# One trunk layer on one core: the unrounded activations rebuilt by a sum, three low parts by transfer instead of four, two weight units split by VectorE, the keys' transposes in other PSUM banks, the rotary tables' products at a later place

## The chip, the cores and the metric

The kernel runs on one core of one Trainium2 chip. The metric is the device time in microseconds of one execution; three runs of the kernel before gave 826.57 (the median), 824.71 and 828.17. All times below are of the kernel before. Engine names are those of the profile: PE is TensorE's matrix multiplication, PEld its load of the stationary operand, DVE is VectorE, ACT ScalarE, POOL GpSimd, and SP the engine whose queue issues most loads.

## The reference

One layer of an encoder over 512 positions of width 1024, in float32. Cut to what matters:

```python
h = rmsnorm(x, pre_mix_g)
aq, ak, av, hq, hf_fwd, hf_bwd, hi, hg = split_columns(h @ w_in, IN_SPLITS)
att = axial_gqa_attention(apply_rope(rmsnorm(aq)), apply_rope(rmsnorm(ak)), av)   # 8 heads of 64, 2 of keys
rec = hgrn2_group(hq, hf_fwd, hf_bwd, hi, hg, lb, out_g)                          # 4 heads, a gated scan both ways
x = x + rmsnorm(concat([att, rec]) @ w_out, post_mix_g)
h = rmsnorm(x, pre_x_g);  m = rmsnorm(mem, mem_norm_g)                            # 256 memory rows
x = x + rmsnorm(memory_cross_attention(h, m, w_xq, w_xkv, w_xo), post_x_g)
h = rmsnorm(x, pre_ffn_g)
u = conv3(h @ w_up) + conv_b                                                      # 1024 -> 2 x 2816
x = x + rmsnorm((silu(u_gate) * u_val) @ w_down, post_ffn_g)
```

## The kernel before, in words

**Products.** A float32 product is put together from three faster ones. Each operand is split into a rounded part "hi" (type fp32r) and a rest "lo", and `mm3` (L243 to L245) issues hi·hi, hi·lo and lo·hi into the same PSUM bank. PSUM has eight banks, handed out by four tags, `b`, `s`, `c`, `o`, two banks each. A tag's third request waits until the first one's bank has been read for the last time.

**Splitting.** `split` (L118, L119) casts the source to hi on ACT and subtracts on DVE. For activations the source is mostly a PSUM bank, so that bank stays taken until DVE's subtraction has read it.

**Weights.** Weights come in units of 128x1024 numbers. `issue` loads a unit into a `raw` buffer on SP's queue and makes its `wh` and `wl`, up to three units ahead of the one that PE uses. For most units that is `split`. For units in `NEG_SCALAR` (7 to 30) ACT casts (L212), ACT writes the negative of the rounded part into `wl` (L214), and a transfer issued by POOL (L217) adds the unit from DRAM on top of it, so DVE has nothing to do there. For units in `NEG_POOL` POOL does the negation (L216). Units 7 to 10 are those of the recurrent group's output gate, `put_sg`, which is the first of `mix_projections`.

**Streams.** `weave` interleaves generators: first the projections (`mix_projections`, with `hgrn_in` for each recurrent head) and the cores of heads 0 to 2 (`hgrn_core`), then the core of head 3 with the self-attention and the cross-attention's key projections. A core goes through its levels: an ACT copy (L604), four small products on PE (L607), two in-place updates on DVE (L633), and a masked copy (L639). Each engine has one fixed order of instructions, made when the kernel is built, and takes them in that order; an instruction that waits holds up all behind it on that engine.

**Rotary tables.** `rope_tables` scales the loaded cosines and sines by the rows' norms (four ACT products, L671) and multiplies them with the gains of queries and keys (four DVE products, L674 and L676). They are first used when the queries are normalized, at 175.5 us. `mem_turn`, the transposition of the normalized memory, ends at about 135 us.

**Keys.** `turn_k(b)` transposes one block of 128 keys on PE (L715) into a bank of tag `b`, from which ACT copies it (L716). The cross-attention's key projections, which run at the same time, also take their banks from `b`. Blocks 0 and 1 are turned after key projection 1, blocks 2 and 3 after key projection 2. The attention's scores (L830) need all four.

**Up-projection.** `between` norms the rows after the cross-attention; its `turn_in` transposes a block of rows into two banks (L282), splits both (L118, L119) and, for this stage only, copies both once more to an unrounded buffer `fulls` (L289). The first two columns' products (`us`) run beside the last transpositions. Later columns i = 5, 8, 11, 14 and 17 go through `strassen_pair`, which needs four sums of quarters of the unrounded input (`sum_of_h`, L1080, and a `split` each), made at i = 2 and 3, one after each product. A pair's four weight units are the loaded `diag` and `side` and two sums of those (`add_blocks`, L188 to L194).

**Down-projection.** Seven products of sums run one after the other, each over three groups of columns. `left_side(p, g)` makes the left operand of product p and group g: for pairs in `NEG_GROUP`, which is group 1 of products 1, 2, 5 and 6, ACT casts (L1022), POOL negates (L1023) and a transfer of POOL's adds the source (L1024); for all others `split` does it. Ahead of product 3 DVE overwrites a source in place (L1014).

Of the kernel before, what the change touches and what calls it, by code (L numbers as in the profile page):

```python
# [9 lines left out]
F32 = mybir.dt.float32  # L10
# [3 lines left out]
ACT = mybir.ActivationFunctionType  # L14
# [4 lines left out]
P = 128  # L19
D = 1024  # L20
T = 512
NB = T // P
# [15 lines left out]
UP_PRODUCTS = ("w11", "w22", "t2", "w21", "t1", "t3", "t4")  # L38
LAY_AHEAD, LOAD_AHEAD = 3, 5
SIDES_AT = (18, 19)  # L40
NEG_GROUP = frozenset((p, 1) for p in (1, 2, 5, 6))
AHEAD = 3
HOLD_BLOCK = 4
TURN_STEP, MEM_TURN, UP_TURN = 0, (0, 4), (0, 2)
NEG_SCALAR = frozenset(range(7, 31))
NEG_POOL = frozenset(range(31, 42))
CORE_SHARE, ATT_LEAD = 53.0, 4.0
KEY_TURNS = {1: (0, 1), 2: (2, 3)}
# [38 lines left out]
def layer(tc, io, out):  # L87
    nc = tc.nc
# [16 lines left out]
    def bank(tag):  # L105
        return ps.tile([P, 512], F32, name="ps_" + tag, tag=tag)

    def big(shape, dt=F32):
        return b8.tile(shape, dt, name="big", tag="big")
# [137 lines left out]
    def blk(b):  # L247
        return slice(b * P, (b + 1) * P)
# [26 lines left out]
        nc.vector.scalar_tensor_tensor(out=h[:, half(c)], in0=xb[:, half(c)], scalar=r, in1=g[:, half(c)],  # L275
                                       op0=ALU.mult, op1=ALU.mult)

    def turn_in(h, act, b, tags, keep=None):
        for c in range(2):
            o = bank(tags[c]).rearrange("p (k n) -> p k n", k=4)  # L280
            for k in range(4):
                nc.tensor.transpose(o[:, k, :], h[:, blk(c * 4 + k)], ident)  # L282
            hi, lo = act.hi, act.lo
            if len(hi) == 2:
                split(hi[c][:, :, blk(b)], lo[c][:, :, blk(b)], o)
            else:
                split(hi[0][:, c * 4:c * 4 + 4, blk(b)], lo[0][:, c * 4:c * 4 + 4, blk(b)], o)
            if keep:
                nc.scalar.copy(keep[c][:, :, blk(b)], o)  # L289

    def row_rstd(xb, h):
        ss = small()
# [13 lines left out]
        nc.vector.scalar_tensor_tensor(out=xb[:, cols], in0=yg, scalar=ss[:, R:R + 1], in1=xb[:, cols],  # L306
                                       op0=ALU.mult, op1=ALU.add)

    def between(x, g_post, g_pre, act, keep=None):
        def first(b, y):  # L310
            ss = small()
            return ss, residual_part(ss, y, g_post, 0, half(0), False, "th")

        def second(b, got, y):
            h = tmp4([P, D])
            ss = small()
            got = got[0], (got[1], residual_part(got[0], y, g_post, 1, half(1), True))
            for c in range(2):
                residual_add(got[0], got[1][c], x[b])
                nc.scalar.activation(h[:, half(c)], x[b][:, half(c)], ACT.Square, accum_out=ss[:, c:c + 1])  # L320
                rstd_part(ss, c, c == 1)
            for c in range(2):
                scale_rows(x[b], ss[:, R:R + 1], g_pre, h, c)
            return lambda: turn_in(h, act, b, y_tags[0][b] + y_tags[1][b], keep)
        return first, second

    def new_act():
# [106 lines left out]
    hT = new_act()  # L434
# [96 lines left out]
    def pair(act, i):  # L531
        t = big([P, 2, 2, T], F32R)
        act.hi[i], act.lo[i] = t[:, 0], t[:, 1]
    sg_box, heads, qkv, rec_done = [], {}, {}, [0]

    def put_v(b, o):
        nc.scalar.mul(v[:, b, :], o, r[:, b:b + 1])
# [17 lines left out]
    def hgrn_in(h, between=()):  # L555
        qk = big([P, 2, 2, T])
        tt = big([P, 2048])
        q = tmp2(tag="tq")

        def put_q(z):  # L560
            nc.scalar.activation(q, z, ACT.Sigmoid)
            nc.vector.tensor_mul(q, z, q)

        def put_f(d):
            def put(z):
                f = tt[:, d * T:(d + 1) * T]
                k = qk[:, 1, d, :]
                nc.scalar.activation(f, z, ACT.Sigmoid)
                nc.scalar.activation(k, z, ACT.Sigmoid, scale=-1.0)
                nc.scalar.activation(f, f, ACT.Identity, scale=oml[:, d, h:h + 1], bias=lb[:, d, h:h + 1])  # L570
                nc.vector.scalar_tensor_tensor(out=qk[:, 0, 1 - d, :], in0=f, scalar=oml[:, d, h:h + 1], in1=q,
                                               op0=ALU.mult, op1=ALU.mult)
            return put

        for put in (put_q, put_f(0), put_f(1)):
            yield from proj_fm(hT, T, "b", scaled(put))
            for job in between[:3]:
                job()
            between = between[3:]
        heads[h] = (q, qk, tt)  # L580
# [86 lines left out]

    def rope_tables():
        rope, cs = qkv["tables"][:, 0:4], qkv["tables"][:, 4:6]
        for b in range(NB):  # L670
            nc.scalar.mul(cs[:, :, b, :], cs[:, :, b, :], r[:, b:b + 1])  # L671
        nc.vector.tensor_scalar(qkg[:, 0, :], qkg[:, 0, :], 0.125, None, op0=ALU.mult)
        for i in range(2):
            nc.vector.tensor_mul(rope[:, 2 * i], cs[:, 0], qkg[:, None, i, :].to_broadcast([P, NB, 64]))  # L674
            gs = pat(qkg, i * 64 + 1, [[0, NB], [2, 32], [-1, 2]])
            nc.vector.tensor_tensor(out=rope[:, 2 * i + 1].rearrange("p b (i two) -> p b i two", two=2),  # L676
                                    in0=cs[:, 1].rearrange("p b (i two) -> p b i two", two=2), in1=gs, op=ALU.mult)
        return rope
# [30 lines left out]
                                in1=kd[:, :, 0].bitcast(F32), op=ALU.subtract)  # L709

    def turn_k(b):
        o = bank("b").rearrange("p (k n) -> p k n", k=4)
        kd4 = qkv["kd"][:, b].rearrange("p a b c d -> p (a b) (c d)")
        for i in range(4):
            nc.tensor.transpose(o[:, i, :].bitcast(F32R), kd4[:, i, :], ident_r)  # L715
        nc.scalar.copy(qkv["kT"][:, :, blk(b)], o)  # L716
# [263 lines left out]

    g_post, g_pre = gains("post_x_g", "pre_ffn_g")
    hT = new_act()
    fulls = [big([P, 4, T]) for _ in range(2)]
    turns = res_second(ox, range(4), kv["x0"], between(x, g_post, g_pre, hT, fulls))

    acts, sides, gates, last_act = [], [], {}, [None]
    half_t = [slice(0, 256), slice(256, 512)]
# [75 lines left out]
    for part in range(2):  # L1063
        cols = slice(part * 256, part * 256 + 256)
        for n in range(4):
            for kc in range(8):
                mm3(us[n][:, cols], (ws[n][0][:, kc, :], ws[n][1][:, kc, :]), hT.get(kc, cols), kc == 0, kc == 7)
            if part:
                conv(*first[n], us[n])
            elif n in UP_TURN:  # L1070
                turns.popleft()()
    wide = [big([P, 2, 4, 256]) for _ in range(2)]
    s1, s2, s3, s4 = wide[0][:, 0], wide[0][:, 1], wide[1][:, 0], wide[1][:, 1]
    (a11, a21), (a12, a22) = [[f[:, :, t] for t in half_t] for f in fulls]
    sums_of_h = [(t[:, 0], t[:, 1]) for t in (big([P, 2, 4, 256], F32R) for _ in range(4))]
    of_h = [(s1, a21, a22), (s2, a11, s1), (s3, a21, a11), (s4, a12, s2)]

    def sum_of_h(k):
        o, i0, i1 = of_h[k]
        nc.vector.tensor_sub(o, i0, i1)  # L1080
        split(*sums_of_h[k], o)
# [43 lines left out]
    for i in range(2, NF):  # L1125
        if i in UP_S:
            strassen_pair(i)
        else:
            for c in range(2):
                o = next_bank()  # L1130
                w = unit(8)
                for kc in range(8):
                    mm3(o, (w[0][:, kc, :], w[1][:, kc, :]), hT.get(kc, slice(0, T)), kc == 0, kc == 7)
                conv(c, i, o)
                if i < 4:
                    sum_of_h(2 * i - 4 + c)
        if i % 3 == 2 and i // 3 < 6:
            new_sums(i // 3)

# [173 lines left out]
```

## Time and profile before

| what | value |
|---|---|
| three runs, median (lowest to highest) | 826.57 us (824.71 to 828.17) |
| the profiled execution | 825.72 us, of it a span of 823.8 us |
| granted TensorE clock, mean | 0.999 |
| busy: PE, PEld | 808.1 us (98%), 690.6 us (84%) |
| busy: DVE, ACT, POOL | 568.5 (69%), 473.0 (57%), 132.3 (16%) us |
| transfers issued by POOL into `wl` (L217) | 35 of 512 KB, 5.4 us to landing (median) |
| copies L289 | 8 of 128x512, 0.59 us each, between 460.3 and 483.2 us |

The span is counted from the first instruction to the last. In a row of the timeline stand the start, the duration, engine, line, operation, tiles and shapes, and in square brackets the idle time of that engine before it with what ended it. In the chain of waits a row is start, duration and what the end of the program was waiting for at that moment.

### The profile page before, as it was taken

To read this page: it belongs to the slowest core of one execution; us is meant where nothing else is said; L and a number is where in the kernel's file an instruction comes from. 1 tells how busy PE (TensorE), PEld (TensorE's weight loads), DVE (VectorE), ACT (ScalarE), POOL (GpSimd) and SP (SyncE) were. 2 spreads that over 40 slices of the span, in tenths; PEclk is the share of its full clock that TensorE was granted. 3 is DMA by queue.
4 is the path that set the end of the run, shared out by engine and by line. 5 is a ranking of instruction groups with operands and counts; after the bars stand their busy time and mean duration, and the time that the engine had idled before them with its cause. 6 is when DMAs were issued, how large, how long until landed. Compare 5 with 4: busy or idle time off the path is not lost.

```text
span 823.8 us, 11495 instructions
## 1 busy us (share of the span) xinstructions
PE 808.1 (98%) x4354; PEld 690.6 (84%) x4354; DVE 568.5 (69%) x849; ACT 473.0 (57%) x785; POOL 132.3 (16%) x194
## 2 busy tenths in 40 slices
PE   9999999999999999999999999999999999999996
PEld 7878888889898887888888898889889888878884
DVE  5347486569886875855453769787687796868865
ACT  6666756369788874645543665444344453556651
POOL 0110211044233101300001300111110102100302
PEclk9999999999999999999999999999999999999999
DMA  9696753657668533252212145787898885368842
GB/s 316 186 283 134 173 112 95 129 140 162 160 155 191 116 136 120 77 179 78 88 43 101 37 163 153 205 232 202 224 279 217 232 250 146 103 200 295 249 124 102
DMA packets 39671, 135.66 MB, mean 165 GB/s; under 512 B 5120, under 2 KB 6656, under 8 KB 39424
## 3 DMA queue, kind: packets, MB, share of 16 engines
q1 hardware_dynamic: 25632, 86.03, 30.0%
q0 software_dynamic: 10960, 40.38, 25.5%
q10 hardware_dynamic: 3024, 8.53, 2.9%
q8 instruction: 34, 0.56, 0.3%
q14 instruction: 21, 0.17, 0.1%
HBM read 130.72 MB, written 25.17 MB: 189 GB/s over the span
## 4 chain that ended last, share of the span: by engine, by line
PE 84%; DMA 4%; DVE 4%; issue 3%; ACT 2%; POOL 2%; SPq 0%; POOLq 0%; DVEq 0%; ACTq 0%
PE ps_b L243 9%; PE ps_b L244 9%; PE ps_b L245 9%; PE ps_s L244 6%; PE ps_s L245 6%; PE ps_s L243 6%; PE ps_o L243 5%; PE ps_o L245 5%; PE ps_o L244 5%; PE ps_c L245 4%; PE ps_c L244 4%; PE ps_c L243 4%; PE ps_c L607 3%; PE ps_o L851 2%; PE ps_s L830 2%
## 5 line engine op out<-in xcount | busy, mean ns | idle before, releaser
L119 DVE TENSOR_TENSOR wl<-raw,wh 128x1024 fp32r<-128x1024 f32 (+1 forms) x75 | 90.7, 1212 | 64.1 <-ACT wh L118 63.8
L118 ACT CAST wh<-raw 128x1024 fp32r<-128x1024 f32 (+1 forms) x75 | 76.8, 1027 | 83.0 <-PE ps_b L244 25.7
L243 PE MATMUL ps_b<-big,wh 128*128 128x512 f32 (+1 forms) x340 | 122.4, 360 | 0.7 <-DVE big L119 0.7
L245 PE MATMUL ps_b<-big,wl 128*128 128x512 f32 (+1 forms) x340 | 120.5, 355 | 0.0
L244 PE MATMUL ps_b<-big,wh 128*128 128x512 f32 (+1 forms) x340 | 120.5, 354 | 0.0
L243 PEld LDWEIGHTS ps_b<-big,wh 128*128 128x128 f32 x340 | 64.3, 189 | 9.2 <-DVE big L119 0.9
L244 PEld LDWEIGHTS ps_b<-big,wh 128*128 128x128 f32 x340 | 64.3, 189 | 8.6
L245 PEld LDWEIGHTS ps_b<-big,wl 128*128 128x128 f32 x340 | 64.2, 189 | 8.7
L633 DVE TENSOR_TENSOR big<-big 128x512 f32<-128x512 f32 x64 | 48.4, 761 | 16.4 <-PE ps_c L607 10.1
L244 PE MATMUL ps_s<-wl,big 128*128 128x512 f32 (+1 forms) x140 | 53.4, 381 | 2.6 <-DVE wl L119 1.7
L243 PE MATMUL ps_s<-wh,big 128*128 128x512 f32 (+1 forms) x140 | 53.5, 384 | 0.4 <-DVE big L119 0.4
L245 PE MATMUL ps_s<-wh,big 128*128 128x512 f32 (+1 forms) x140 | 53.1, 379 | 0.0
L212 ACT CAST wh<-raw 128x1024 fp32r<-128x1024 f32 x35 | 36.8, 1052 | 26.7 <-PE ps_b L244 12.9
L217 POOL DMA_DIRECT2D wl<-in_w_dram x35 | 30.9, 883 | 120.1 <-ACT wl L214 105.1
L119 DVE TENSOR_TENSOR big<-ps_o,big 128x512 fp32r<-128x512 f32 x54 | 37.0, 688 | 14.1 <-ACT big L118 12.2
L998 POOL DMA_DIRECT2D sum_t<-in_wd_dram x24 | 19.7, 833 | 143.7 <-DMA sum_t<-in_wd_dram 86.8
L118 ACT CAST big<-ps_o 128x512 fp32r<-128x512 f32 x54 | 31.6, 589 | 17.2 <-PE ps_o L953 7.5
L243 PE MATMUL ps_o<-wh,big 128*128 128x512 f32 (+1 forms) x102 | 39.3, 386 | 0.0
L244 PE MATMUL ps_o<-wl,big 128*128 128x512 f32 (+1 forms) x102 | 38.2, 375 | 0.0
L245 PE MATMUL ps_o<-wh,big 128*128 128x512 f32 (+1 forms) x102 | 38.2, 374 | 0.0
L244 PE MATMUL ps_c<-big,wh 128*128 128x256 f32 (+1 forms) x112 | 37.6, 336 | 0.0
L243 PE MATMUL ps_c<-big,wh 128*128 128x256 f32 (+1 forms) x112 | 37.6, 336 | 0.0
(311 smaller groups left out, 2171.0 us busy)
## 6 DMA issues: line engine op xcount, KB each, us to landing
raw<-in_w_dram SPq DMA_DIRECT2D x85, 512.0 KB, 3.3
wl<-in_w_dram POOLq DMA_DIRECT2D x35, 512.0 KB, 5.4
sum_t<-in_wd_dram POOLq DMA_DIRECT2D x20, 512.0 KB, 8.1
tmp<-in_w_dram SPq DMA_DIRECT2D x14, 512.0 KB, 6.0
sum_t<-in_wd_dram ACTq DMA_DIRECT2D x10, 512.0 KB, 6.2
sum_t<-sum_t POOLq DMA_DIRECT2D x10, 512.0 KB, 5.2
big<-sum_t SPq DMA_DIRECT2D x10, 512.0 KB, 4.9
raw<-sum_t SPq DMA_DIRECT2D x10, 512.0 KB, 4.5
```

The lines of the kernel that those rows point to most:

```text
L118: nc.scalar.copy(hi, src)
L119: (eng or nc.vector).tensor_sub(lo, src, hi.bitcast(F32))
L212: nc.scalar.copy(wh, raw)
L217: nc.gpsimd.dma_start(wl, io["w"][i], accum_op=ALU.add)
L243: nc.tensor.matmul(o, a[0], b[0], start=start, stop=False, skip_group_check=again)
L244: nc.tensor.matmul(o, a[0], b[1], start=False, stop=False, skip_group_check=again)
L245: last_mm[0] = nc.tensor.matmul(o, a[1], b[0], start=False, stop=stop, skip_group_check=again).ins
L607: nc.tensor.matmul(o[:, b, :], kc[:, blk(b)], pat(qk, b * P, [[2 * m, P // (2 * m)], [T + m, 2], [1, m]]), start=True, stop=True)
L633: nc.vector.tensor_tensor(out=c, in0=c, in1=pat(tt, toff + off, [[2, npair], [gap, 2], [0, m]]), op=ALU.mult)
L830: nc.tensor.matmul(s, qT[h // 4][:, h % 4, blk(qb)], kT[:, 2 * (h // 4) + c, :], start=c == 0, stop=c == 1)
L851: nc.tensor.matmul(o, vv[:, c, h // 4].rearrange("p a d -> p (a d)"), pt[j][:, c, :], start=c + j == 0, stop=c == 3 and j == 1)
L998: nc.gpsimd.dma_start(t, weight_block(second_name, width(u)), accum_op=ALU.add)
```

## The change

Five edits go together:

- `turn_in` no longer copies to `fulls`; `full_h(c)` makes each half of `fulls` later by one DVE sum of the hi and lo parts, 128x2048, at i = 2. The four `sum_of_h` all move to i = 3, two after each product.
- `NEG_GROUP` loses product 1, so that its group 1 is split by ACT and DVE.
- `NEG_SCALAR` begins at 9, so that units 7 and 8 are split by ACT and DVE.
- The four ACT products of the rotary tables are recorded behind the newest forget gate's last activation (L570), and DVE's four follow them.
- `turn_k` takes its bank from the tags `s`, `s`, `o`, `o` of the blocks' own projections.

```diff
-NEG_GROUP = frozenset((p, 1) for p in (1, 2, 5, 6))
+NEG_GROUP = frozenset((p, 1) for p in (2, 5, 6))
...
-NEG_SCALAR = frozenset(range(7, 31))
+NEG_SCALAR = frozenset(range(9, 31))
...
     def turn_in(h, act, b, tags, keep=None):          # loses the argument keep
...
-            if keep:
-                nc.scalar.copy(keep[c][:, :, blk(b)], o)
...
-                nc.scalar.activation(f, f, ACT.Identity, scale=oml[:, d, h:h + 1], bias=lb[:, d, h:h + 1])
+                last_gate[0] = nc.scalar.activation(f, f, ACT.Identity, scale=oml[:, d, h:h + 1],
+                                                    bias=lb[:, d, h:h + 1]).ins
...
-        for b in range(NB):
-            nc.scalar.mul(cs[:, :, b, :], cs[:, :, b, :], r[:, b:b + 1])
+        with tc.issue_after(last_gate[0]):
+            for b in range(NB):
+                nc.scalar.mul(cs[:, :, b, :], cs[:, :, b, :], r[:, b:b + 1])
...
     def turn_k(b):
-        o = bank("b").rearrange("p (k n) -> p k n", k=4)
+        o = bank(tm_tags[b]).rearrange("p (k n) -> p k n", k=4)
...
+    def full_h(k):
+        nc.vector.tensor_add(fulls[k], hT.hi[k].bitcast(F32), hT.lo[k].bitcast(F32))
...
                 conv(c, i, o)
-                if i < 4:
-                    sum_of_h(2 * i - 4 + c)
+                if i == 2:
+                    full_h(c)
+                elif i == 3:
+                    sum_of_h(2 * c)
+                    sum_of_h(2 * c + 1)
```

The buffers `fulls` are now taken behind the first two columns instead of ahead of them. The edits also shift line numbers: in the changed file L606 is the line that was L607, L603 that was L604, L1079 is `full_h`, L1083 the sum in `sum_of_h` that was L1080, and L1039, L1041 and L1052 the convolution's lines that were L1040, L1042 and L1053.

On PE, around the keys' transposes, the order before is this, from the end of key projection 1 (L243 to L245) to the start of projection 2, and then from the end of projection 2 to the scores, with part of projection 3 left out between:

```order
L245 MATMUL ps_b<-big,wl 128x256
L715 MATMUL ps_b<-ident_r,big 128x128 x4
L607 MATMUL ps_c<-big,tmp_1932 128x128 x4
L715 MATMUL ps_b<-ident_r,big 128x128 x4
L243 MATMUL ps_b<-big,wh 128x256
...
L715 MATMUL ps_b<-ident_r,big 128x128 x4
L607 MATMUL ps_c<-big,tmp_2090 128x128 x4
L715 MATMUL ps_b<-ident_r,big 128x128 x4
...
L830 MATMUL ps_s<-big 128x512 x4
```

And this is the same stretch of PE's order in the changed kernel:

```order
L245 MATMUL ps_b<-big,wl 128x256
L715 MATMUL ps_s<-ident_r,big 128x128 x6
L606 MATMUL ps_c<-big,tmp_1930 128x128 x4
L715 MATMUL ps_s<-ident_r,big 128x128 x2
L243 MATMUL ps_b<-big,wh 128x256
...
L715 MATMUL ps_o<-ident_r,big 128x128 x8
...
L830 MATMUL ps_s<-big 128x512 x4
...
L606 MATMUL ps_c<-big,tmp_2088 128x128 x4
```

The transposes left tag `b` and stand closer together; the core's small products that stood between the second pair of blocks now follow the scores.

On DVE, at the columns i = 2 and 3 of the up-projection, the order before begins with the end of column 1's convolution (L1053) and goes on with the sums of quarters (L1080), their low parts (L119 to `big`), the weights' low parts (L119 to `wl`) and the weights' sums (L188, L190):

```order
L1053 TENSOR_TENSOR big<-tmp_4663,tmp_4692 128x512
L1080 TENSOR_TENSOR big<-big 128x1024
L188 TENSOR_TENSOR both<-raw 128x1024
L1040 SCALAR_TENSOR_TENSOR tmp_4734<-ps_b,cw,tmp_4734 128x511
L119 TENSOR_TENSOR wl<-tmp_4445,wh 128x1024
L1042 SCALAR_TENSOR_TENSOR tmp_4734<-ps_b,cw,tmp_4734 128x511
L119 TENSOR_TENSOR big<-big 128x1024
...
L194 TENSOR_TENSOR tmp_4877<-raw 128x512
L1053 TENSOR_TENSOR big<-tmp_4824,tmp_4864 128x512
L119 TENSOR_TENSOR wl<-both,wh 128x1024
```

The changed kernel's DVE has there, from the same convolution on:

```order
L1052 TENSOR_TENSOR big<-tmp_4651,tmp_4680 128x512
L1079 TENSOR_TENSOR big<-big 128x2048
L1039 SCALAR_TENSOR_TENSOR tmp_4724<-ps_b,cw,tmp_4724 128x511
L119 TENSOR_TENSOR wl<-tmp_4437,wh 128x1024
L1041 SCALAR_TENSOR_TENSOR tmp_4724<-ps_b,cw,tmp_4724 128x511
L1079 TENSOR_TENSOR big<-big 128x2048
L188 TENSOR_TENSOR both<-raw 128x1024
...
L1083 TENSOR_TENSOR big<-big 128x1024
L1052 TENSOR_TENSOR big<-tmp_4810,tmp_4853 128x512
L119 TENSOR_TENSOR big<-big 128x1024 x2
L119 TENSOR_TENSOR wl<-raw,wh 128x1024
L194 TENSOR_TENSOR tmp_4869<-raw 128x512
```

The two long sums came in ahead of everything else at i = 2, and the last sums' low parts now stand behind column 3's convolution, ahead of the `side` unit's low part and of L194.

On ACT, the rotary products stand before between copies of the first core, at the profile's 64 us:

```order
L604 COPY tmp_540<-big 128x512
L214 ACTIVATE wl<-wh 128x1024
L604 COPY tmp_557<-big 128x512
L671 ACTIVATE big<-big,rx 128x2x64 x4
L604 COPY tmp_580<-big 128x512
```

In the changed kernel ACT has them behind the casts of the turned memory (L118), in front of the copies of the core of head 2 (L597 and L603, which were L598 and L604):

```order
L118 CAST big<-ps_o 128x4x128
L671 ACTIVATE big<-big,rx 128x2x64 x4
L214 ACTIVATE wl<-wh 128x1024
L122 ACTIVATE big<-ps_c,og 128x512
L597 COPY big<-ps_c 128x4x128
L603 COPY tmp_1208<-big 128x512
```

DVE's four products moved with them, from between the first core's updates to behind the low parts of the turned memory. On PE the first L607 of that core stands five products later than before, 17 instead of 12 behind the core's first products (L597).

More of the change, by code (lines that the diff above doesn't have):

```diff
@@ L276, in scale_rows, with turn_in @@
                                        op0=ALU.mult, op1=ALU.mult)
-    def turn_in(h, act, b, tags, keep=None):
+    def turn_in(h, act, b, tags):
         for c in range(2):
@@ L307, in residual_add, with between @@
                                        op0=ALU.mult, op1=ALU.add)
-    def between(x, g_post, g_pre, act, keep=None):
+    def between(x, g_post, g_pre, act):
         def first(b, y):
@@ L323, in second @@
                 scale_rows(x[b], ss[:, R:R + 1], g_pre, h, c)
-            return lambda: turn_in(h, act, b, y_tags[0][b] + y_tags[1][b], keep)
+            return lambda: turn_in(h, act, b, y_tags[0][b] + y_tags[1][b])
         return first, second
@@ L533, in pair @@
         act.hi[i], act.lo[i] = t[:, 0], t[:, 1]
-    sg_box, heads, qkv, rec_done = [], {}, {}, [0]
+    sg_box, heads, qkv, rec_done, last_gate = [], {}, {}, [0], [None]
     def put_v(b, o):
@@ L982, in layer @@
     hT = new_act()
-    fulls = [big([P, 4, T]) for _ in range(2)]
-    turns = res_second(ox, range(4), kv["x0"], between(x, g_post, g_pre, hT, fulls))
+    turns = res_second(ox, range(4), kv["x0"], between(x, g_post, g_pre, hT))
     acts, sides, gates, last_act = [], [], {}, [None]
@@ L1071, in layer @@
                 turns.popleft()()
+    fulls = [big([P, 4, T]) for _ in range(2)]
     wide = [big([P, 2, 4, 256]) for _ in range(2)]
```

## The prediction, made before the changed kernel was run

> **What bounds the kernel now.** I read the page first, for the span, the busy shares and the chain that ended last.
>
> ```profile
> span 823.8 us, 11495 instructions
> PE 808.1 (98%) x4354; PEld 690.6 (84%) x4354; DVE 568.5 (69%) x849; ACT 473.0 (57%) x785; POOL 132.3 (16%) x194
> PE 84%; DMA 4%; DVE 4%; issue 3%; ACT 2%; POOL 2%; SPq 0%; POOLq 0%; DVEq 0%; ACTq 0%
> ```
>
> PE is busy for 98% of the span and carries 84% of the chain. The change takes no product off PE; it can gain only where PE waits. So I went through PE's timeline for starts later than the usual step, which is 0.23 us from one 128x512 matmul to the next (52.08 and 52.31 below) and 0.12 for 128x256, and then read the other engines and the chain of waits around each. "Excess" below is the start minus the previous start minus that step. Five of the longer gaps lie at the edits' places, and each edit has its own.
>
> **Units 7 and 8 split by DVE.** The timeline of PE, ACT, POOL and DVE, and one piece of the chain of waits (start, length, what):
>
> ```profile
> 39.46 0.69 DVE L542 TENSOR_TENSOR tmp<-ps_b,big 128x512 f32<-128x512 f32 x1 [3.55 <-PE ps_b L245]
> 41.70 1.04 ACT L214 ACTIVATE wl<-wh 128x1024 fp32r<-128x1024 f32 x1
> 44.00 0.75 DVE L571 SCALAR_TENSOR_TENSOR big<-big,oml,tmp 128x512 f32<-128x512 f32 x1 [2.95 <-ACT big L570]
> ...
> 43.06 8.41 DMA wl<-in_w_dram
> ...
> 50.14 0.39 PE L243 MATMUL ps_s<-wh,big 128*128 128x512 f32 x1
> 51.52 0.50 PE L244 MATMUL ps_s<-wl,big 128*128 128x512 f32 x1 [0.98 <-DMA wl<-in_w_dram]
> 52.08 0.40 PE L243 MATMUL ps_s<-wh,big 128*128 128x512 f32 x1
> 52.31 0.40 PE L244 MATMUL ps_s<-wl,big 128*128 128x512 f32 x1
> ```
>
> PE stood from 50.37 to 51.52 (excess 51.52 - 50.14 - 0.23 = 1.15) for the low part of unit 8, whose transfer took 8.41 us. The change replaces ACT's 1.04 us and the transfer, for two units, by a 128x1024 subtraction on DVE (1.22 us, the row at 730.37 below). DVE idles 3.55 us ahead of 39.46 and 2.95 ahead of 44.00, which covers one each; unit 8's low part is then there by about 43, 8 us early. If that cover were gone, the subtractions would delay the gates behind them by 2.4 us, less than those 8. POOL's queue and the transfers lose 1 MB, so the next unit's part comes no later. Gain between 0.4 (the next unit's transfer ends last in its place) and 1.15; I take 1.0. A rule of the Trainium skill speaks against this term: "DMA: Bandwidth & Descriptors", section on the anatomy of one DMA on the gpsimd path, gives about 2.0 us plus the bytes at 436 GB/s, an estimate of 3.2 us for 512 KB. By it neither this wait nor that of product 1 below would exist; the rows of 8.41 and 8.46 us decide against it, and what it would give is the fourth rival.
>
> **Product 1's low part by DVE.** Timeline and one piece of the chain:
>
> ```profile
> 717.64 1.94 POOL L1023 TENSOR_SCALAR big<-big 128x1024 fp32r<-128x1024 f32 x1 [17.22 <-ACT big L1022]
> 718.59 1.53 DVE L119 TENSOR_TENSOR wl<-raw,wh 128x512 fp32r<-128x512 f32 x1
> 719.88 8.46 DMA big<-big
> 722.31 1.21 DVE L119 TENSOR_TENSOR wl<-big,wh 128x1024 fp32r<-128x1024 f32 x1
> 728.36 1.23 DVE L1014 TENSOR_TENSOR big<-big 128x1024 f32<-128x1024 f32 x1 [4.83 <-DMA big<-big]
> 729.50 0.95 DVE L119 TENSOR_TENSOR big<-big 128x768 fp32r<-128x768 f32 x1
> 730.37 1.22 DVE L119 TENSOR_TENSOR wl<-raw,wh 128x1024 fp32r<-128x1024 f32 x1
> 731.64 0.50 PE L244 MATMUL ps_s<-wl,big 128*128 128x512 f32 x1 [1.66 <-DVE wl L119]
> ```
>
> DVE's update in place at 728.36 had to wait until the transfer had read its source, and behind it stood the weights' low part that PE wanted at 729.8. In the changed order one more 1.22 us subtraction stands on DVE and the wait is gone: from 722.31 with 1.13 us from one such row to the next, three of them and one of 0.87 more, the weights' low part is ready near 727, about 3 us early. PE's excess here is 1.82, of it 1.66 idle. Bounds 0.8 (another transfer of the same queue ends late) and 1.82; I take 1.8, since nothing but that wait held DVE.
>
> **Keys' transposes in other banks.** PE and ACT:
>
> ```profile
> 208.64 0.54 PE L715 MATMUL ps_b<-ident_r,big 128*128 128x128 f32 x4 [0.22 <-ACT big L716]
> 209.93 0.39 PE L243 MATMUL ps_b<-big,wh 128*128 128x256 f32 x1 [0.75 <-DVE big L119]
> 213.88 1.05 ACT L212 CAST wh<-raw 128x1024 fp32r<-128x1024 f32 x1
> 215.74 0.54 PE L715 MATMUL ps_b<-ident_r,big 128*128 128x128 f32 x4 [0.51 <-ACT big L716]
> 216.31 0.59 ACT L716 CAST big<-ps_b 128x512 fp32r<-128x512 f32 x1
> ```
>
> With both transposes and the projection on tag `b`, PE waited three times for a bank: excess 0.39, 0.88 and 0.67, together 1.94. In `s` and `o` the banks are those of blocks normalized long before, and the `b` bank that projection 2 takes was last read for projection 0. New is that the scores come sooner behind the last transposes: by the order 13 products of 0.12, 1.56 us, stand between, while ACT has two copies of 0.59 to do and, if its cast of 1.05 stands ahead as at 213.88, needs 2.2. A wait of some 0.6 can come of that, and at worst the last of the three comes back with it, so the gain lies between 0.7 and 1.94; I take 1.8.
>
> **Unrounded input by a sum.** ACT, PE, DVE, with the chain's first such piece at 463.54:
>
> ```profile
> 463.54 0.55 ACT big L289
> ...
> 468.93 0.59 ACT L289 COPY big<-ps_b 128x512 f32<-128x512 f32 x1
> 469.53 0.59 ACT L289 COPY big<-ps_s 128x512 f32<-128x512 f32 x1
> 479.06 0.66 PE L282 MATMUL ps_c<-ident,tmp 128*128 128x128 f32 x4 [0.48 <-ACT big L289]
> 479.43 0.69 DVE L119 TENSOR_TENSOR big<-ps_o,big 128x512 fp32r<-128x512 f32 x1
> 480.15 0.59 ACT L289 COPY big<-ps_o 128x512 f32<-128x512 f32 x1 [1.15 <-DVE big L119]
> 480.79 0.39 PE L243 MATMUL ps_o<-big,wh 128*128 128x256 f32 x1 [0.64 <-ACT big L289]
> ...
> 519.93 1.22 DVE L119 TENSOR_TENSOR big<-big 128x1024 fp32r<-128x1024 f32 x1
> 529.38 0.28 PE L243 MATMUL ps_b<-big,wh 128*128 128x256 f32 x1
> 530.82 0.28 PE L243 MATMUL ps_o<-big,wh 128*128 128x256 f32 x1
> ```
>
> PE's excess is 0.64 at 479.06 and 0.80 at 480.79, each for a bank that the copy L289 still held. Without the copies both banks come free with DVE's L119. That alone gives 0.64, since at 480.15 DVE had just finished the second one; the rest comes only if DVE's own work is earlier, and the chain shows that it is: a copy of 0.55 at 463.54 and 1.18 at 468.93 to 470.12 stand in it ahead of the norm's square (L299). Bounds 0.64 and 1.44; I take 1.35.
>
> The price is two sums of 128x2048, which no row shows. From 0.69 for 512 and 1.22 for 1024 elements a row (479.43 and 519.93), 2048 extends to 1.22 + 2 x 0.53 = 2.28; as four of the slowest 128x512 row, 1.53 at 718.59 beside POOL's L1023, it would be 6.1. I take 2.28, 4.56 for both, since POOL computes little here. The Trainium skill ("VectorE: DVE Perf Modes", section on the TRN2 errata) has 2.291 us measured for this sum, and the total would stay the same by it. The busy time by engine in that stretch (length, then PE, PEld, DVE, ACT, POOL):
>
> ```profile
> 499.60:523.10 23.50, 23.50 (x105) 19.47 (x104) 23.30 (x26) 12.69 (x15) 2.27 (x3) 1.00 0.69 198
> ```
>
> DVE has no gap in it, so all behind the sums is 4.56 later. The last sum's low part, ended at 521.15, ends at 525.7; PE first reads it with the second product of the first Strassen pair, at 529.38. The `side` unit's low part now stands right behind it, to 526.9, and is read from 530.82 on. With some 4 us left on both, I cost the edit nothing. Were the cover gone, PE would wait for what exceeds those 4.
>
> **Rotary products behind the last gate.** ACT, DVE, PE:
>
> ```profile
> 64.32 1.28 ACT L671 ACTIVATE big<-big,rx 128x128 f32<-128x128 f32 x4
> 70.17 0.42 DVE L674 TENSOR_TENSOR big<-big,qkg 128x256 f32<-128x256 f32 x1
> 136.41 0.90 ACT L604 COPY tmp<-big 128x512 f32<-128x512 f32 x1
> 137.41 1.53 PE L607 MATMUL ps_c<-big,tmp 128*128 128x128 f32 x8
> 140.28 0.96 PE L607 MATMUL ps_c<-big,tmp 128*128 128x128 f32 x6
> ```
>
> At 64 us the products delay nobody on PE, so their leaving gains nothing. At their new place they put 1.28 us ahead of the copy at 136.41, on which PE's L607 at 137.41 hangs with no slack; PE's order gives back five products, 5 x 0.23 = 1.13. DVE's four, about 1.4 us, delay the update that the second L607 needs: some 0.3 of new wait there. Bounds 0 and -1.3 (order giving nothing back); I take -0.3.
>
> **The sum.** 1.0 + 1.8 + 1.8 + 1.35 - 0.3 = 5.65, off the profiled execution's 825.72: 820.07. The median of the runs is 0.85 above that execution; with half of this added, 820.5.
>
> **The rivals.** Half a per cent, 4.1 us, is about what a measurement of this kernel can tell from no change; from the median that is 822.4.
>
> First: each edit removes its wait, but the next one stands close behind. The scores wait for ACT behind L212 (0.7 left), the second bank at 480 stays with DVE (0.64), L607 at 137 loses 1.3, and other transfers end late (0.4 and 0.8): the lower bounds sum to 1.25, and halfway to mine it is 3.45, so 822.3 to 824.5. For it speaks that DVE is full at 500 and that ACT's work at 205 to 218 is in a fixed order; against it, that the waits read above name the very instruction or transfer that goes.
>
> Second, slower: DVE's backlog at 500 to 526. If its instructions there stretched by the ratio of 1.53 to 0.69 at 718.59, the 25 us between the first long sum and the last low part would grow by 30, and PE would wait 26: about 846. It decides from a stretch of 1.4 on, where 25 x 0.4 = 10 us, less the 4 left, eat the 5.65. Against it: POOL is busy for 2.27 us of that stretch, and DVE's row of 1.22 at 519.93 is not stretched.
>
> Third: an edit does nothing, because a wait for several semaphores hid another one under the one that I read, most likely at unit 8 (the transfer of unit 9 takes its place) or behind product 1 (a load for the same weights): 821.5 or 822.3.
>
> Fourth: the transfers at 43.06 and 719.88 were in truth done some 5 us sooner, and PE's gaps at 51.52 and 731.64 had another cause, which stays: 2.8 less, 823.3. Against it: the chain gives both transfers 8.4 us, up to just before the waiting engine starts. This is what the rule above on the gpsimd path would make of the time.
>
> **How the numbers follow.** My sum within its bounds 0.60; the first rival 0.20; the third 0.10, of which two thirds would still be faster by over half a per cent; the second 0.04; the fourth 0.02; a slower outcome of another kind, such as a core of the woven part that runs late all the way, 0.04. Low end: all upper bounds (1.15 + 1.82 + 1.94 + 1.44 - 0 = 6.35, so 819.4) and the runs' scatter of 1.9 below the median on part of it, 818.0. High end: 825.5, nearly no gain; what lies above is the second rival and the other slower ones. Faster 0.66, same 0.28, slower 0.06.
>
> **What would show it.** Right: no gap over 0.3 at PE's second product of unit 8, at the first products of key projections 2 and 3, at L282 and the first `ps_o` product of the up-projection's second half, nor behind product 1; the first Strassen pair starts without a wait. Wrong: PE waiting at about 525 for `wl` or `big` from DVE; scores waiting for L716; a longer L607 wait at 132 to 136; a transfer named where it was not.

## The result, and the profile after

The changed kernel takes 819.87 us (median of four runs, 819.45 to 820.07); the kernel before took 826.14 in the four runs beside it (824.71 to 828.17). The ratio is 0.9922, 95% interval 0.990 to 0.9943: faster by 0.8%. The forecast was 820.5, between 818.0 and 825.5. The profiled execution took 820.07 us against 825.72, which is 5.65 less.

The head of the page and the chain's shares by engine; the mean granted clock is 0.999, as before:

```profile
span 818.3 us, 11482 instructions
PE 807.5 (99%) x4354; PEld 690.6 (84%) x4354; DVE 574.2 (70%) x854; ACT 467.7 (57%) x775; POOL 127.0 (16%) x190
PE 95%; DVE 2%; ACT 1%; DMA 0%; POOL 0%; issue 0%; POOLq 0%; DVEq 0%; ACTq 0%
```

PE's busy time is the same to 0.6 us, and DVE has 5.7 us more work. What changed is the chain that ended last: PE carries 95% of it instead of 84%, and DMA's 4% are gone.

PE's rows at four of the five places, in order of time: unit 8's second product, the core of head 2, the keys' transposes and the scores (with two rows of ACT), and the last transposes of the up-projection's input.

```profile
50.75 0.39 PE L243 MATMUL ps_s<-wh,big 128*128 128x512 f32 x1
50.98 0.39 PE L244 MATMUL ps_s<-wl,big 128*128 128x512 f32 x1
...
138.12 1.59 PE L606 MATMUL ps_c<-big,tmp 128*128 128x128 f32 x8
141.07 1.20 PE L606 MATMUL ps_c<-big,tmp 128*128 128x128 f32 x8 [0.20 <-ACT wh L212]
...
206.29 0.62 PE L715 MATMUL ps_s<-ident_r,big 128*128 128x128 f32 x6
207.04 1.23 PE L606 MATMUL ps_c<-big,tmp 128*128 128x128 f32 x8
208.02 0.38 PE L715 MATMUL ps_s<-ident_r,big 128*128 128x128 f32 x2
208.23 0.35 PE L243 MATMUL ps_b<-big,wh 128*128 128x256 f32 x1
212.20 0.80 PE L715 MATMUL ps_o<-ident_r,big 128*128 128x128 f32 x8
212.28 1.06 ACT L212 CAST wh<-raw 128x1024 fp32r<-128x1024 f32 x1
213.50 1.07 ACT L716 CAST big<-ps_o 128x512 fp32r<-128x512 f32 x2
214.63 1.20 PE L830 MATMUL ps_s<-big 128*128 128x512 f32 x4
...
476.13 0.60 PE L282 MATMUL ps_c<-ident,tmp 128*128 128x128 f32 x4
476.57 0.60 PE L282 MATMUL ps_o<-ident,tmp 128*128 128x128 f32 x4
477.12 0.36 PE L243 MATMUL ps_o<-big,wh 128*128 128x256 f32 x1
```

Of the waits that the prediction quoted, the brackets are gone at unit 8 (50.75 to 50.98 is the usual step), at all L715, at the first product of key projection 2 (208.23), at L282 and at the `ps_o` product behind it. One small bracket is new, 0.20 at 141.07.

DVE behind product 1 with PE's product that waited there before, and DVE with PE at the up-projection's first Strassen pair:

```profile
717.75 1.22 DVE L119 TENSOR_TENSOR wl<-big,wh 128x1024 fp32r<-128x1024 f32 x1
718.89 1.22 DVE L1013 TENSOR_TENSOR big<-big 128x1024 f32<-128x1024 f32 x1
720.02 0.95 DVE L119 TENSOR_TENSOR big<-big 128x768 fp32r<-128x768 f32 x1
720.89 1.22 DVE L119 TENSOR_TENSOR wl<-raw,wh 128x1024 fp32r<-128x1024 f32 x1
726.12 0.39 PE L244 MATMUL ps_s<-wl,big 128*128 128x512 f32 x1
...
496.56 2.29 DVE L1079 TENSOR_TENSOR big<-big 128x2048 f32<-128x2048 f32 x1
501.25 2.28 DVE L1079 TENSOR_TENSOR big<-big 128x2048 f32<-128x2048 f32 x1
520.83 1.22 DVE L119 TENSOR_TENSOR big<-big 128x1024 fp32r<-128x1024 f32 x1 [0.18 <-ACT big L118]
521.97 1.22 DVE L119 TENSOR_TENSOR wl<-raw,wh 128x1024 fp32r<-128x1024 f32 x1
...
525.69 0.28 PE L243 MATMUL ps_b<-big,wh 128*128 128x256 f32 x1
527.13 0.28 PE L243 MATMUL ps_o<-big,wh 128*128 128x256 f32 x1
```

The in-place update follows its neighbours without a bracket, and the weights' low part, done at 722.11, is 4.0 us ahead of PE's product. The long sums took 2.29 and 2.28 us. The last sum's low part ended at 522.05 and PE's product that reads it began at 525.69; the `side` unit's ended at 523.19 for 527.13. Some 3.6 and 3.9 us were left.

### The profile page after: what moved, and what is told of

It reads as the page before. It is cut to its first block, busy times and chain, and to the rows that moved or that the text cites. A ratio compares the mean times of both kernels' runs of the same rounds, so it can differ in the third digit from the quotient of the medians.

```text
span 818.3 us, 11482 instructions
## 1 busy us (share of the span) xinstructions
PE 807.5 (99%) x4354; PEld 690.6 (84%) x4354; DVE 574.2 (70%) x854; ACT 467.7 (57%) x775; POOL 127.0 (16%) x190
## 4 chain that ended last, share of the span: by engine, by line
PE 95%; DVE 2%; ACT 1%; DMA 0%; POOL 0%; issue 0%; POOLq 0%; DVEq 0%; ACTq 0%
PE ps_b L244 10%; PE ps_b L245 10%; PE ps_b L243 10%; PE ps_s L244 7%; PE ps_s L245 7%; PE ps_s L243 7%; PE ps_o L243 5%; PE ps_o L244 5%; PE ps_o L245 5%; PE ps_c L243 4%; PE ps_c L244 4%; PE ps_c L245 4%; PE ps_c L606 3%; PE ps_o L851 2%; PE ps_s L830 2%; PE ps_o L840 2%
## 5 line engine op out<-in xcount | busy, mean ns | idle before, releaser
L119 DVE TENSOR_TENSOR wl<-raw,wh 128x1024 fp32r<-128x1024 f32 (+1 forms) x77 | 92.2, 1200 | 65.9 <-ACT wh L118 65.8
L118 ACT CAST wh<-raw 128x1024 fp32r<-128x1024 f32 (+1 forms) x77 | 79.0, 1028 | 85.1 <-PE ps_b L244 21.8
L243 PE MATMUL ps_b<-big,wh 128*128 128x512 f32 (+1 forms) x340 | 122.4, 360 | 0.0
L245 PE MATMUL ps_b<-big,wl 128*128 128x512 f32 (+1 forms) x340 | 120.6, 355 | 0.0
L245 PEld LDWEIGHTS ps_b<-big,wl 128*128 128x128 f32 x340 | 64.2, 189 | 8.7
L243 PEld LDWEIGHTS ps_b<-big,wh 128*128 128x128 f32 x340 | 64.3, 189 | 8.4
L243 PE MATMUL ps_s<-wh,big 128*128 128x512 f32 (+1 forms) x140 | 53.2, 381 | 0.4 <-DVE big L119 0.4
L245 PE MATMUL ps_s<-wh,big 128*128 128x512 f32 (+1 forms) x140 | 53.0, 379 | 0.0
L212 ACT CAST wh<-raw 128x1024 fp32r<-128x1024 f32 x33 | 34.7, 1053 | 23.8 <-PE ps_b L244 12.8
L119 DVE TENSOR_TENSOR big<-ps_o,big 128x512 fp32r<-128x512 f32 x54 | 37.0, 687 | 14.3 <-ACT big L118 12.6
L118 ACT CAST big<-ps_o 128x512 fp32r<-128x512 f32 x54 | 31.7, 588 | 16.8 <-PE ps_o L953 7.5
L243 PE MATMUL ps_o<-wh,big 128*128 128x512 f32 (+1 forms) x102 | 39.2, 385 | 0.0
L245 PE MATMUL ps_o<-wh,big 128*128 128x512 f32 (+1 forms) x102 | 38.4, 377 | 0.0
L243 PE MATMUL ps_c<-big,wh 128*128 128x256 f32 (+1 forms) x112 | 37.6, 336 | 0.0
```

What stands on the lines that cost most here:

```text
L118: nc.scalar.copy(hi, src)
L119: (eng or nc.vector).tensor_sub(lo, src, hi.bitcast(F32))
L212: nc.scalar.copy(wh, raw)
L243: nc.tensor.matmul(o, a[0], b[0], start=start, stop=False, skip_group_check=again)
L245: last_mm[0] = nc.tensor.matmul(o, a[1], b[0], start=False, stop=stop, skip_group_check=again).ins
```

## The experiments

Five of these kernels each take one of the edits back out of the changed kernel; most of the others vary one of them. "Ratio" is to the kernel before, run beside it, with its 95% interval; the changed kernel has 0.9922. Gaps are read from PE's rows as in the prediction: the bracket is PE's idle time, the excess is the delay against the usual step. A time "above the changed kernel" is the difference of the two medians; these come from different sets of runs, beside which the kernel before had medians from 825.19 to 826.68, so such a difference is good to some 1.5 us, and the gaps say more.

### Units 7 and 8 by transfer again

```diff
-NEG_SCALAR = frozenset(range(9, 31))
+NEG_SCALAR = frozenset(range(7, 31))
```

> The changed kernel, but units 7 and 8 again by ACT and a transfer. Theory (five separate waits, each worth its own gap on PE): the gap for the low part of unit 8 comes back, 1.0 to 1.15 us behind the start of that unit, all else stays; time 819.9 + 1.0 = 820.9. Rival (the waits hide each other): the gap does not come back or another grows, time within 0.3 us of 819.9.

Measured: 821.64 us (820.40 to 823.68, six runs), ratio 0.9944 (0.9926 to 0.9962). The profile is of the longest of the six. In it the gap is back, twice as long as in the kernel before. PE's row and the stretches around it (length, then the busy time of PE, PEld, DVE, ACT and POOL, the granted clock, the DMA share and GB/s):

```profile
52.88 0.50 PE L244 MATMUL ps_s<-wl,big 128*128 128x512 f32 x1 [2.09 <-DMA wl<-in_w_dram]
52.00:54.00 2.00, 1.12 (x4) 0.94 (x5) 1.14 (x1) 0.43 (x1) 0.85 (x1) 0.87 1.03 283
54.00:56.00 2.00, 2.00 (x7) 1.52 (x6) 0.00 (x0) 0.84 (x1) 0.00 (x0) 0.50 1.03 330
56.00:58.00 2.00, 2.00 (x8) 1.61 (x7) 0.00 (x0) 0.20 (x1) 0.00 (x0) 0.78 1.07 326
```

The theory stands, and the price of this wait was under-estimated: the transfer took 9.52 us here, against 8.41 in the profile of before. Landing later, it makes a gap of 2 us instead of 1, and behind the longer one PE was granted half its clock for a while. How often that happens, the one profile does not show; the median is 1.8 above the changed kernel, the shortest of the six 0.5.

### Unit 8 alone by transfer

```diff
-NEG_SCALAR = frozenset(range(9, 31))
+NEG_SCALAR = frozenset(range(8, 31))
```

> The changed kernel, but unit 8 again by ACT and a transfer, and unit 7 still by DVE. Theory (the transfer takes 8.4 us because the queues are full at 43 to 51): with one transfer of 512 KB less it lands 0 to 1.5 us earlier than 51.5, and PE's gap is 0 to 1.1. Rival (a rule of about 3.2 us for 512 KB, with another cause for the gap): it lands near 47, and a gap of 1.1 comes back all the same.

Measured: 820.35 us (one run). The chain's piece and PE's row:

```profile
41.92 9.22 DMA wl<-in_w_dram
51.18 0.50 PE L244 MATMUL ps_s<-wl,big 128*128 128x512 f32 x1 [0.46 <-DMA wl<-in_w_dram]
```

The transfer took 9.22 us, no less than with its neighbour in flight; it was issued 1.14 us sooner and so landed 0.33 sooner. That it comes from the one neighbour falls; that it takes about 3 us falls by far. PE's gap of 0.46 is in the expected span. That full queues are the reason is not shown: the DMA engines' share was 0.83 to 1.07 in stretches of 2 us between 42 and 52 us here and 0.92 to 1.05 in the kernel before, so they were busy in both.

### Product 1's low part by transfer again

```diff
-NEG_GROUP = frozenset((p, 1) for p in (2, 5, 6))
+NEG_GROUP = frozenset((p, 1) for p in (1, 2, 5, 6))
```

> The changed kernel, but product 1's low part again by POOL and a transfer. Theory: DVE waits some 5 us for that transfer at its update in place, and PE's gap behind it comes back with 1.8 to 2.0 us; time 821.8. Rival (a load for the same weights would have ended as late): PE's gap is under 1.0 us, time under 820.9.

Measured: 821.82 us (820.96 to 821.87), ratio 0.9942 (0.9925 to 0.9959), 1.95 above the changed kernel.

```profile
724.66 1.23 DVE L1013 TENSOR_TENSOR big<-big 128x1024 f32<-128x1024 f32 x1 [4.89 <-DMA big<-big]
727.95 0.50 PE L244 MATMUL ps_s<-wl,big 128*128 128x512 f32 x1 [1.73 <-DVE wl L119]
```

DVE waits 4.89 us for the transfer, PE 1.73 for DVE, an excess of 1.89: the theory, to a tenth.

### The keys' transposes in tag b again

```diff
-        o = bank(tm_tags[b]).rearrange("p (k n) -> p k n", k=4)
+        o = bank("b").rearrange("p (k n) -> p k n", k=4)
```

> The changed kernel, but the keys' transposes again in tag b. Theory: the three gaps for banks come back, with the shortened one at L606 in front of them 2.1 us more of PE gaps between 200 and 220 us; time 822.0. Rival (the place of the scores in the order made the gain, not the banks): the gaps come back with less than 1.0.

Measured: 822.43 us (821.12 to 823.42), ratio 0.9952 (0.9933 to 0.9971), 2.6 above the changed kernel. All four brackets are back, with the kernel before's lengths, 1.86 together, so the rival's "less than 1.0" is excluded. In the profiled execution the clock fell behind them (last row, the same columns as above): it is one of two that took 823.4 us at a mean granted clock of 0.995; the other two took 821.1 and 821.5 at 0.999 and 0.997.

```profile
206.84 1.20 PE L606 MATMUL ps_c<-big,tmp 128*128 128x128 f32 x8 [0.37 <-DVE tmp L697]
208.26 0.54 PE L715 MATMUL ps_b<-ident_r,big 128*128 128x128 f32 x4 [0.22 <-ACT big L716]
209.55 0.58 PE L243 MATMUL ps_b<-big,wh 128*128 128x256 f32 x1 [0.75 <-DVE big L119]
216.83 0.54 PE L715 MATMUL ps_b<-ident_r,big 128*128 128x128 f32 x4 [0.52 <-ACT big L716]
210.00:212.00 2.00, 2.00 (x11) 2.00 (x11) 1.39 (x5) 0.62 (x1) 0.00 (x0) 0.50 1.05 244
```

### The copies of the unrounded input again, all of them, and by halves

The first kernel has the copies L289 and the sums at i = 2 and 3 as before:

```diff
+            if keep:
+                nc.scalar.copy(keep[c][:, :, blk(b)], o)
...
-                if i == 2:
-                    full_h(c)
-                elif i == 3:
-                    sum_of_h(2 * c)
-                    sum_of_h(2 * c + 1)
+                if i < 4:
+                    sum_of_h(2 * i - 4 + c)
```

> The changed kernel, but with the copies L289 and the sums of quarters at i = 2 and 3 as before. Theory: 1.4 to 1.5 us of gaps come back between 465 and 485 us, nothing at 520; time 821.3. Rival (only the last bank's copy counts): 0.64 comes back, time 820.5.

Measured: 820.85 us (820.81 to 821.27), ratio 0.9935 (0.992 to 0.995), 0.98 above the changed kernel. Both brackets are back (0.47 and 0.64), with the excess of the kernel before (0.63 + 0.79 = 1.42), as the theory said; the time is 0.5 shorter than the 821.3 expected. The other two kernels keep `full_h` and only add the copies as extra work, in one for the blocks of rows 0 and 1, in the other for 2 and 3:

```diff
+            if keep and b in (0, 1):      # the other: (2, 3)
+                nc.scalar.copy(keep[c][:, :, blk(b)], o)
```

> The changed kernel with ACT's copies of the unrounded input put back for the first two blocks of rows only (extra work; the sums overwrite them). Theory (these four copies stand in the chain that sets when DVE does the last block): PE has no gap at the last transposes but 0.6 to 0.8 at the product behind them, time 820.6. Rival (only the copies that hold a bank at that moment count): no gap, 819.9.

> The same, but the copies put back for the last two blocks of rows only. Theory: the chain ahead stays short, the banks come free in time despite the copies, PE's gaps together stay under 0.4, time 820.1. Rival (the held bank alone): 1.4 of gaps come back, 821.3.

Measured: 820.53 and 819.84 us (one run each). PE's rows with brackets from 474 to 479 us, of all copies (two rows), of the first blocks' and of the last blocks':

```profile
476.39 0.66 PE L282 MATMUL ps_c<-ident,tmp 128*128 128x128 f32 x4 [0.47 <-ACT big L289]
478.13 0.38 PE L243 MATMUL ps_o<-big,wh 128*128 128x256 f32 x1 [0.64 <-ACT big L289]
```

```profile
477.84 0.36 PE L243 MATMUL ps_o<-big,wh 128*128 128x256 f32 x1 [0.73 <-ACT big L118]
```

```profile
477.10 0.39 PE L243 MATMUL ps_o<-big,wh 128*128 128x256 f32 x1 [0.48 <-ACT big L289]
```

Neither theory had both right. The first blocks' copies, which hold no bank that PE waits for, make a gap of 0.73 by way of the chain. The last blocks' make 0.48 by holding the bank, more than the theory's 0.4 and a third of the rival's 1.4; this gap is seen in the row alone, since the time lies within the changed kernel's own runs. Together they give 1.21 of idle time, and all copies 0.47 + 0.64 = 1.11.

### The rotary products at their old place

```diff
-        with tc.issue_after(last_gate[0]):
-            for b in range(NB):
-                nc.scalar.mul(cs[:, :, b, :], cs[:, :, b, :], r[:, b:b + 1])
+        for b in range(NB):
+            nc.scalar.mul(cs[:, :, b, :], cs[:, :, b, :], r[:, b:b + 1])
```

> The changed kernel, but the rotary tables' products at their old place. Theory: this edit alone cost time, through DVE's and ACT's products ahead of the core of head 2; PE's gaps between 130 and 145 us shrink by 0.3 and nothing appears at 60 to 80, so 819.6 and the fastest of all. Rival: the products delay the first core where they stood, and the edit was worth something: a gap of 0.3 or more appears between 55 and 80 us, 820.2.

Measured: 822.76 us (820.36 to 824.19, six runs), ratio 0.9947 (0.9927 to 0.9967): by the medians 2.9 longer than the changed kernel, by the ratios 2.1, where 0.3 shorter was expected. ACT and PE:

```profile
61.17 0.69 ACT L670 ACTIVATE big<-big,rx 128x128 f32<-128x128 f32 x2 [3.96 <-DMA big<-in_rope_dram]
62.42 1.78 PE L606 MATMUL ps_c<-big,tmp 128*128 128x128 f32 x8 [2.36 <-ACT tmp L603]
64.00:66.00 2.00, 2.00 (x6) 1.61 (x6) 1.76 (x3) 1.38 (x3) 0.86 (x1) 0.50 0.71 260
```

Without the negations of units 7 and 8 on ACT, the fixed order has two of the four products two copies of the first core (L603) earlier than in the kernel before. The next section's kernel has them at the same place. There ACT meets them 3.96 us before the tables have landed, PE waits 2.36 for the copy behind them, and the clock falls. In the profile of the kernel before the tables landed at 62.9 (15.3 us after their issue), and the products at 64.32 were safe by 1.4 us. The rival had the place right, a wait of the first core, but 820.2 for its time, and 0.3 or more for a gap of 2.36.

### One edit alone on the kernel before

```diff
-NEG_SCALAR = frozenset(range(7, 31))
+NEG_SCALAR = frozenset(range(9, 31))
```

> The kernel before with one edit alone: units 7 and 8 split by DVE. Theory (found in the run with the rotary products at their old place): without ACT's two negations the fixed order moves the rotary products ahead of a copy of the first core, and there they wait for the tables' transfer, which lands near 61; so PE's gap of 1.1 for unit 8 goes, one of about 2.4 comes at the first core, and the time is 1.2 us longer than before, 827.5, in some executions more, with a lower clock behind the gap. Rival (the sum of the prediction, edits add up): 1.0 shorter, 825.3.

Measured: 828.13 us (823.92 to 830.98, ten runs), the kernel before 825.19 beside it, ratio 1.0029 (1.0011 to 1.0047). The edit that is worth 1.15 us in the sum makes the kernel slower when it comes alone. The profile is of the shortest of the ten executions, in which the tables landed early and ACT's wait was short:

```profile
58.57 0.69 ACT L671 ACTIVATE big<-big,rx 128x128 f32<-128x128 f32 x2 [1.45 <-DMA big<-in_rope_dram]
```

PE had no gap there. ACT was ready for the tables at 57.1. In the fourteen profiles of this document they land between 56.6 and 63.7, and only once before 57.1. That the longer executions are those with a later landing, as in the run above, is inferred and not seen in a profile of this kernel; their mean granted clock is on record, 0.993 to 0.996 in the five that took over 828 us and 0.997 to 0.999 in the other five.

### The rotary products 12 us earlier

```diff
-                last_gate[0] = nc.scalar.activation(f, f, ACT.Identity, scale=oml[:, d, h:h + 1],
-                                                    bias=lb[:, d, h:h + 1]).ins
+                gate = nc.scalar.activation(f, f, ACT.Identity, scale=oml[:, d, h:h + 1], bias=lb[:, d, h:h + 1]).ins
+                if d == 0:
+                    last_gate[0] = gate
```

> The changed kernel, but the rotary products recorded behind the forward gate of head 2 instead of the newest gate, about 12 us earlier, where ACT idles 2.6 and DVE 5.3 us. Theory: PE's gaps between 130 and 145 us lose 0.3 against the changed kernel, nothing else comes: 819.6, the fastest. Rival (the 0.3 there comes from the core's own chain of updates, whatever ACT does): same gaps, 819.9.

Measured: 819.31 us (818.86 to 819.50, five runs), ratio 0.993 (0.9916 to 0.9943). The products now fill ACT's and DVE's idle time, and the second small product of head 2's core has no bracket; L607 here is the changed kernel's L606.

```profile
122.13 0.69 ACT L672 ACTIVATE big<-big,rx 128x128 f32<-128x128 f32 x2
123.76 0.42 DVE L675 TENSOR_TENSOR big<-big,qkg 128x256 f32<-128x256 f32 x1 [0.75 <-ACT big L672]
139.12 1.20 PE L607 MATMUL ps_c<-big,tmp 128*128 128x128 f32 x8
```

The gap of 0.20 is gone as the theory says. By time it is the shortest kernel of all, yet it ran beside shorter runs of the kernel before (825.19), and its ratio does not differ from the changed kernel's. That a wait of 0.20 is gone is shown; that the kernel is faster than the changed one is not.

### How much room DVE has at i = 2

```diff
-        nc.vector.tensor_add(fulls[k], hT.hi[k].bitcast(F32), hT.lo[k].bitcast(F32))
+        for _ in range(2):      # the other: 4
+            nc.vector.tensor_add(fulls[k], hT.hi[k].bitcast(F32), hT.lo[k].bitcast(F32))
```

> Each of the two long sums is made twice, 4.57 us more of DVE at i = 2; the result is the same. The changed kernel's timeline has the last sum's low part done at 522.05 for a PE product at about 523.9. Theory from that row: only 2 us are left, so PE waits 2.5 to 2.8 at the first Strassen pair, time 822.5. By the prediction's margin of 4 us: PE waits 0.6, time 820.5. If DVE were no bound there: no wait, 819.9.

> Each of the two long sums is made four times, 13.7 us more of DVE at i = 2; the result is the same. Theory: the wait on PE is 13.7 less the 2 us left, 11.8, and the time 831.7, slower than the kernel before. By the prediction's margin of 4: 9.7, 829.6. If the backlog were made good before the first pair: under 825.

Measured: 819.43 and 830.70 us (one run each). With twice the sums no PE row between 524 and 527 us names a releaser; three steps there (starts at 524.80, 525.22, 525.49 and 525.71) are longer than 0.12, by 0.55 together. With four times:

```profile
525.70 0.39 PE L245 MATMUL ps_c<-big,wl 128*128 128x256 f32 x1 [1.05 <-DVE wl L119]
530.30 0.58 PE L243 MATMUL ps_o<-big,wh 128*128 128x256 f32 x1 [3.15 <-ACT wh L118]
533.83 0.58 PE L243 MATMUL ps_b<-big,wh 128*128 128x256 f32 x1 [2.30 <-ACT big L118]
532.00:536.00 4.00, 1.56 (x5) 1.27 (x6) 4.00 (x4) 1.19 (x2) 0.80 (x1) 0.50 0.63 124
```

The theory with 2 us of room was a misreading: PE's product was put at 523.9, too early by the 1.8 us that product 1 gains only 200 us later. The row is at 525.69. By the prediction's 4 us, 0.6 and 9.7 were expected; 0.55 and, in time over the changed kernel, 10.8 were found, the last with a stretch of half clock in it. That the 0.55 agrees is partly luck. With the longer queue the build gives PE and DVE another order: the step at 525.22 waited for ACT's cast of the last sum (524.13 + 1.04 = 525.17), not for its low part; this was done at 526.43, and other products had been put ahead of its first reader, at 527.02. A backlog there does make the kernel slower than before, as the second rival said, but only from somewhere between 4.6 us of added work (819.43) and 13.7 (830.70). These two runs bound the room and do not measure it.

## Why the prediction was right, and where it was not

**The sum.** 5.65 us were predicted and 5.65 measured between the profiled executions, though partly by luck. By the excess of the quoted rows the five places gave what the table says. The first of the four terms of the keys' row is a wait of the kernel before that the prediction did not list:

```profile
207.22 1.20 PE L607 MATMUL ps_c<-big,tmp 128*128 128x128 f32 x8 [0.37 <-DVE tmp L697]
```

| term | predicted | gap before | gap after | gain |
|---|---|---|---|---|
| units 7 and 8 | 1.0 | 1.15 | none | 1.15 |
| product 1 | 1.8 | 1.82 | none | 1.82 |
| keys' banks, with the L607 ahead of them | 1.8 | 0.50 + 0.39 + 0.88 + 0.67 | 0.26 | 2.18 |
| unrounded input | 1.35 | 0.64 + 0.80 | none | 1.44 |
| rotary products | -0.3 | 0.13 | 0.36 | -0.23 |
| sum | 5.65 | | | 6.36 |

The 0.7 between 6.36 and 5.65 lies almost all ahead of the first of these waits: unit 8's first product started at 50.75 in the profiled execution and at 50.14 in that of before. That start moves from one execution to the next: over the twelve profiled variants it lies between 49.76 and 50.73. The earliest is the kernel with doubled sums, whose order is the changed kernel's up to there:

```profile
49.76 0.39 PE L243 MATMUL ps_s<-wh,big 128*128 128x512 f32 x1
```

So the waits gave 0.7 more than was forecast, and a later start took it back.

**Step by step.** Units 7 and 8: right; no transfer took the place of the one that left. Product 1: right, with the weights' low part done 4.0 us early where 3 were forecast. Keys: under-sized by 0.4, since the scores did not wait for ACT (no bracket at 214.63) although its cast of 1.05 did stand ahead of the last two copies, and the two transposes moved ahead of L607 took half of its wait. It was close: the cast began at 212.28, while PE was still at the transposes, and the copies ended at 214.57, 0.06 ahead of the scores. The forecast had counted the whole cast behind the transposes. Unrounded input: right by the rows, and in both halves of its reason, the held bank and the chain, by the two halves' runs; the kernel with the copies back is only 0.98 longer, which by itself is inside the noise. The price of 2.28 for a long sum: measured 2.29 and 2.28, and the room of some 4 us as estimated. Head 2's core: right in size and in its reason. The bracket at 141.07 names a cast of ACT's that the product does not read; what it reads is DVE's update:

```profile
139.75 1.17 DVE L632 TENSOR_TENSOR big<-big 128x512 f32<-128x512 f32 x1
```

The update ends at 140.92, 0.15 ahead of the product. In the kernel before the same update ended 0.14 ahead of it (138.98 + 1.16, then 140.28).

**The step that failed.** "At 64 us the products delay nobody on PE, so their leaving gains nothing" was read from the order of before, and the other edits change that order. In the changed kernel the old place would have cost 2 to 3 us, so the move is worth that much there, and the units' edit without it is a loss. The sum came out right because it compared only the two orders that exist, where the rotary products wait in neither; the prices of the single edits do not add. Taken back one at a time, the five cost 1.8, 2.0, 2.6, 1.0 and 2.9 us by the medians, some 10 together, against 6.3 for the whole change; stretches of half clock are in these prices too.

**The rivals.** The first (new waits behind the old ones) took 0.2 us at 141.07 and no more. The second did not come up; its threshold lies inside what the two runs with longer sums bracket and was not measured. The third did not come up. The fourth is excluded: both gaps went with their transfers and came back with them, and the transfer of unit 8 alone took 9.22 us.

## What to carry to other kernels

When PE is nearly always busy, list the starts that are late against its usual step, and read for each what the waiting row names; each gap that an edit takes away then shows up in the time, about one for one here (an excess of 1.89 us for 1.95 of time in one kernel, 1.42 for 0.98 in another). Price edits together and not singly where a fixed order is made from all of them: taking two instructions off an engine can pull others forward into a wait for a load that they had been safe from. A long operation on a full engine costs nothing up to the room left at its first reader, so find that reader's row and subtract.

## What the runs showed of the hardware that was not expected

PE gaps well under 3 us are followed, in some executions, by about 3.4 us at half the granted clock. It was seen behind one gap of 2.09 us (clock 0.87, 0.50 and 0.78 in three stretches of 2 us, so 2 x (0.13 + 0.50 + 0.22) = 1.7 us lost, twice that at half clock), behind one of 2.36, and behind three of 0.37, 0.22 and 0.75 within 3 us. Cut at its ends the stretch runs from 53.47 to 56.88, from 62.77 to 66.19 and from 209.54 to 212.95, each time at a granted clock of 0.50; with the fourfold sums it runs from 529.39 to 539.63, three times as long, and begins inside the gap of 3.15. It was not seen in the profiled executions behind 1.66 and 1.73 us, and not behind the same three gaps in the kernel before. What decides between the two stays open. The Trainium skill ("TensorE: Matmul & The Clock Gate", Part 1 on the HAM clock gate) has the clock decided in free-running windows of about 3.4 us, and the array slowed behind a window of idling; the length agrees, but the gaps here are shorter than a window. A gap on PE thus costs its length and sometimes 1.7 us more. That fits the spread of the runs, 824.71 to 828.17 before and 819.45 to 820.07 after the gaps were gone. It also fits their clocks: of nine runs of the kernel before beside the first experiments, the three longest (826.87 to 828.48) have a mean granted clock of 0.995 and the others 0.997 to 0.999. No profile of the longer runs of before was taken.

A transfer of 512 KB issued by POOL took 8.41, 9.22 and 9.52 us from issue to landing between 42 and 53 us, that of 9.22 with one transfer fewer of its kind ahead of it. The rotary tables' 256 KB were issued between 46.9 and 47.9 us in all fourteen profiles and took 8.9 to 15.8 us to land; they landed just before 58.57 in one profile and 61.17 in another where ACT waited for them, so a fixed order that is safe in one execution waits in the next.
